# A macaron encoder block: the third chunk of the second feed-forward in two token spans, preloaded function tables, other load rates in the ordering model

## The chip, the cores and the metric

The kernel runs on one core of a Trainium2 chip. The metric is the device time of one execution in microseconds (us). TensorE (PE) multiplies, VectorE (DVE), ScalarE (ACT) and GpSimd (POOL) do the rest, SyncE (SP) issues most of the DMA transfers. Each engine takes its instructions in a fixed order.

## The reference

One layer of a bidirectional encoder on 512 tokens of width 1024, in float32. Two feed-forwards of half weight stand around a mixer of two attention groups, each between two RMS norms.

```python
def swiglu(h, w_gu, w_down):
    gate, up = jnp.split(h @ w_gu, 2, axis=-1)      # 1024 -> 2 x 2816
    return (jax.nn.silu(gate) * up) @ w_down        # 2816 -> 1024

f = swiglu(rms_norm(h, ffn1_pre_g), ffn1_w_gu, ffn1_w_down)
h = h + 0.5 * rms_norm(f, ffn1_post_g)
z = rms_norm(h, mix_pre_g) @ w_in
q_na, k_na, v_na, c_q, c_kv, k_rope = jnp.split(z, split_at, axis=-1)
o_na = neighbourhood_attention(q_na, k_na, v_na, na_rpb)           # 8 heads of 64
o_mla = latent_attention(c_q, c_kv, k_rope, ..., cos, sin)          # 8 heads, softmax over 512 keys
mixed = concatenate([rms_norm(o_na, na_out_norm_g), rms_norm(o_mla, mla_out_norm_g)]) @ w_out
h = h + rms_norm(mixed, mix_post_g)
f = swiglu(rms_norm(h, ffn2_pre_g), ffn2_w_gu, ffn2_w_down)
h = h + 0.5 * rms_norm(f, ffn2_post_g)
```

## The kernel before

**Numbers as pairs.** Every matrix operand is held as two parts, hi (rounded to the matmul's type) and lo (the rest). `split` (line 333) makes them: ScalarE copies to hi, VectorE or GpSimd subtracts to lo. `load_w` (342) loads a weight tile of 128 x 1024 into one of three staging tiles (the ring `raws`) and splits it into a ring of four hi and four lo tiles (`his`, `los`), unless a place is given in `to`. `mm3` (351) makes three matmuls of each product: hi hi, hi lo, lo hi.

**The feed-forward.** `ffn` (392) is called twice. Its 22 chunks of 128 hidden columns each have a gate half (u = 0) and an up half (u = 1). The first `direct` chunks (six in the first call, three in the second) are computed directly by `gate_up` (405), each half into its own PSUM bank, (4 + 2c + u) mod 8, over a list of token spans; the others by `winograd` (460), with fewer products on sums of quarters, whose operands `operands` (434) prepares. Then the products come back through DRAM and `down` (535) multiplies them with the second weight. `load_gu` (399) loads and splits a chunk's two weight tiles. `after` (499) adds what follows a chunk: the next chunk's weights, the sums for the Winograd part, its first operands. In the first call the tokens are there from the start, and the row norms of x are worked out beside chunks 0 and 1: four loads of token tiles, squares on ScalarE, an inverse root on GpSimd and a small matmul with a diagonal for each (lines 678 to 686). In the second call chunks 0 and 1 run over two spans, tokens 256 to 511 first, then 0 to 255; the other chunks take all 512 tokens in one matmul.

**Between mixer and second feed-forward.** The queries and keys of the latent attention lie in `Q_AT` (793) and `kbuf`. `mla_pair(j, hf)` (1041) does heads 2j and 2j + 1 for half of the tokens. Then `w_out_b` (1102) does the second half of the output projection for one token tile n, in the order 2, 3, 0, 1; its product goes to two PSUM banks (from bank 5 on, for tile 1 from bank 0 on). The norm chain that follows is: scale and add (VectorE), square with a sum (ScalarE, into a scratch area in memory), inverse root (GpSimd), multiply, scale and add, a second square and root, scale, then eight transposes on TensorE (`put_xT`, 374) and a split.

**The order.** Nothing is issued directly. `Plan.add` (111) records each operation with its dependencies, found from the addresses that it reads and writes, and with a modelled duration: for a DMA its bytes over a rate that depends on the run length, for a matmul its columns, for the other engines a fixed part and a part for each column. `Plan.place` (151) is a list scheduler forwards and backwards over these costs, with a lock between VectorE and GpSimd operations on SBUF, a slower TensorE after a long idle time, and a limit on SP's backlog of DMA. `Plan.issue` (220) repeats it six times and emits the operations in the order of the best modelled start times. So any change of a cost can move any instruction.

Of the kernel before, what the change touches and what calls it, by code (L numbers as in the profile page):

```python
# [14 lines left out]
AF = mybir.ActivationFunctionType  # L15
# [5 lines left out]
S = 512  # L21
# [6 lines left out]
EPS = 1e-6  # L28
# [15 lines left out]
class Plan:  # L44
# [66 lines left out]
    def add(self, eng, op, a, k):  # L111
        is_ap = lambda x: hasattr(x, "ap") and hasattr(x, "offset")
        outs = [x for x in (*a[:1], k.get("out"), k.get("accum_out")) if x is not None and is_ap(x)]
        ins = [x for x in (*a[1:], *(v for n, v in k.items() if n not in ("out", "accum_out"))) if is_ap(x)]
        n, deps = len(self.ops), set()
        for x in ins:
            for key, runs in self.runs(x):
                for lo, hi in runs:
                    self.touch(n, key, lo, hi, key[0] == "psum", deps)
        for x in outs:  # L120
            for key, runs in self.runs(x):
                for lo, hi in runs:
                    self.touch(n, key, lo, hi, True, deps)
        cols = max(math.prod(c for _, c in list(x.ap)[1:]) for x in outs[:1] + ins)
        kind = lambda x: x.tensor.name.rsplit("_", 1)[0]
        size = math.prod(c for _, c in list(outs[0].ap))
        big = [x for x in ins if math.prod(c for _, c in list(x.ap)[1:]) > 1]
        in_sb = sum(kind(x) != "psum" for x in big)
        tail, lock, dma = self.TAIL.get(eng, 0), False, 0
        if op == "dma_start":  # L130
            run = min(list(x.ap)[-1][1] for x in (outs[0], ins[0]))
            dma = 4 * size / (380 if run >= 1024 else 320 if run >= 512 else 230 if run >= 256 else 180 if run >= 128 else 60)
            busy, tail = (330 if eng == "SP" else 400 if eng == "ACT" else 1000), 0
        elif eng == "PE":
            busy = max(109, (cols + 32) / 2.4) * (1 + (op == "matmul" and a[1].dtype == F32))
            tail += cols / 2.4 - busy
        else:
            fix, per = {"ACT": (190, 0.834) if in_sb else (132, 0.872), "DVE": (140, 1.045), "POOL": (90, 1.0)}[eng]
            if ALU.pow in a:
                fix, per = 390, 160  # L140
            elif eng == "POOL" and in_sb > 1:
                fix, per = (130, 2.2) if cols > 256 else (300, 1.2)
            fix += 90 * (AF.Exp in a) + 45 * (op == "scalar_tensor_tensor")
            if k.get("accum_out") is not None:
                fix += 195 if eng == "ACT" else 75
            busy = fix + per * cols - tail
            in_psum = sum(kind(x) == "psum" for x in big + outs)
            lock = in_sb > 1 or in_sb and (eng == "POOL" or not in_psum and eng == "DVE")
        self.ops.append((eng, op, a, k, deps, busy, tail, lock, dma))
# [92 lines left out]
def r_(ap):  # L242
    return ap.bitcast(F32R)
# [3 lines left out]
def hybrid_block(ctx, tc, A, out):  # L247
    nc = tc.nc
    plan = Plan(tc)
    ACT, DVE, POOL, PE, SP = (plan.engine(e) for e in ("ACT", "DVE", "POOL", "PE", "SP"))  # L250
# [38 lines left out]
    gbuf, scr = big[:, :2048], big[:, 2048:]  # L289
# [6 lines left out]
    bst = Ring([new(8) for _ in range(8)])  # L296
# [8 lines left out]
    def reg(o, n):  # L305
        assert R0 + o + n <= NCOL - N32
        return mem[:, R0 + o : R0 + o + n]
# [34 lines left out]
    def load_w(src, n=1024, eng=DVE, raw=None, to=None):  # L342
        raw = fetch(src, n) if raw is None else raw
        hi, lo = to or (his.get()[:, :n], los.get()[:, :n])
        split(hi, lo, raw, eng)
        return hi, lo
# [14 lines left out]
    def row_rms(src, scratch, scale, eps, st=stat):  # L361
        s = st.get()
        ACT.activation(scratch, src, AF.Square, scale=scale, accum_out=s[:, 0:1])
        DVE.tensor_scalar(s[:, 1:2], s[:, 0:1], eps, None, ALU.add)
        return rstd(s[:, 1:2], st)
# [26 lines left out]
    def ffn(w_gu, w_dn, gpost, on_tile, L, first, resid, mid_tile=None, rs=None):  # L392
# [6 lines left out]
        def load_gu(c):  # L399
            for u in range(2):  # L400
                i = 2 * c + u
                hi, lo = load_w(w_gu[i])
                ws[c, u] = (hi.rearrange("p (k j) -> p k j", k=KD), lo.rearrange("p (k j) -> p k j", k=KD))

        def gate_up(cs, spans, nxt):
            pb = {(c, u): bank((4 + 2 * c + u) % 8) for c in cs for u in range(2)}
            for i, (t0, t1) in enumerate(spans):
                for c in cs:
                    order = [(k, u) for u in range(2) for k in range(KD)]
                    for k, u in sorted(order) if c in by_k else order:  # L410
                        wh, wl = ws[c, u]
                        mm3(pb[c, u][:, t0:t1], (wh[:, k, :], wl[:, k, :]), xt(k, t0, t1),
                            k == 0 and i == 0, k == KD - 1 and i == len(spans) - 1)
            nxt()
            for c in cs:
                tm = L["tmp"].get()
                sil, g = tm[:, :512], tm[:, 512:]
                if rs is None:
                    ACT.activation(sil, pb[c, 0], AF.Silu)
                else:  # L420
                    DVE.tensor_tensor(sil, pb[c, 0], rs, ALU.mult)
                    ACT.activation(sil, sil, AF.Silu)
                    DVE.tensor_tensor(sil, sil, rs, ALU.mult)
                DVE.tensor_tensor(g, pb[c, 1], sil, ALU.mult)
                SP.dma_start(gdr[c], g)
# [73 lines left out]
        def after(c):  # L499

            if 0 < c < direct - 1:
                load_gu(c + 1)
            for f in steps.get(c, ()):
                f()
            if c == direct - 1:
                operands(direct)

        by_k = ()
        if rs is None:
            load_gu(0)  # L510
            load_gu(1)
            gate_up((0, 1), [(t, t + 256) for t in first], lambda: after(1))
        else:
            ws, by_k = first, (0, 1)
            gate_up((0,), [(0, S)], lambda: after(0))
            gate_up((1,), [(0, S)], lambda: after(1))
        for c in range(2, direct):
            gate_up((c,), [(0, S)], lambda: after(c))
        for c in range(direct, NFC):
            winograd(c)  # L520


        slots, last_w = ([reg(o, 1024) for o in x] for x in (L["slots"], L["last_w"]))
# [39 lines left out]
        for n in range(NT):  # L563
            s = stat.get()
            t = ts.get()
# [152 lines left out]
    def scale(k):  # L718
# [9 lines left out]
    L1 = {  # L728
        "tmp": Ring([h[0], h[1]]), "sums": (hall[:, :2048], hall[:, 2048:]),
        "sets": (reg(22528, 7168), reg(0, 7168), his_los), "B": B1, "steps": steps1, "direct": 6,  # L730
        "order": lambda c: 1 if c < 8 else (c + 1) % 2,
        "slots": [1024 * i for i in range(7)] + [8192 + 1024 * i for i in range(6)]
        + [26624 + 1024 * i for i in range(4)] + [7168] + [14336 + 1024 * i for i in range(4)],
# [368 lines left out]
    def w_out_b(n, b0, hr):  # L1102
        t = slice(n * P, (n + 1) * P)
        mx = h[n]
        SP.dma_start(hr, h1[n * P : (n + 1) * P, :])
        ps = psum[:, b0 * 512 : b0 * 512 + 1024]
        for j in range(4):
            oh, ol = oT[4 + j]
            for hf in range(2):
                c = slice(hf * 512, hf * 512 + 512)  # L1110
                mm3(ps[:, c], (oh[:, t], ol[:, t]), (wb[j][0][hf], wb[j][1][hf]), j == 0, j == 3)
        DVE.scalar_tensor_tensor(mx, ps, rB[:, n : n + 1], mx, ALU.mult, ALU.add)
        sq = reg(Q_AT[6] + 256, 1)
        sq = r_(bass.AP(tensor=sq.tensor, offset=sq.offset, ap=[sq.ap[0], [Q_AT[4] - Q_AT[6], 2], [512, 2], [1, 256]]))
        r = row_rms(mx.rearrange("p (a b c) -> p a b c", a=2, b=2), sq, 1.0 / 32, EPS, bst)
        DVE.tensor_tensor(mx, mx, gp, ALU.mult)
        DVE.scalar_tensor_tensor(mx, mx, r, hr, ALU.mult, ALU.add)
        SP.dma_start(h2[n * P : (n + 1) * P, :], mx)
        r = row_rms(mx.rearrange("p (a b c) -> p a b c", a=2, b=2), sq, 1.0 / 32, EPS, bst)
        DVE.scalar_tensor_tensor(hr, mx, r, gn, ALU.mult, ALU.mult)  # L1120
        put_xT(n, hr, (2, 3), mx)

# [20 lines left out]
    w_out_b(2, 5, raws.get())  # L1143
    mla_pair(3, 0)
    w_out_b(3, 5, raws.get())
    o_rstd(1, (0, 1))
    w_out_b(0, 5, tmps.get())
    w_out_b(1, 0, tmps.get())
# [2 lines left out]
    def after2(n, t):  # L1151
# [11 lines left out]
    L2 = {  # L1163
        "tmp": cut(1024, 3), "sums": (hall[:, :2048], gbuf),
        "sets": (reg(12288, 7168), reg(19456, 7168), his_los), "B": B2, "steps": steps2, "direct": 3,
        "order": lambda c: c % 2,
        "slots": [19456 + 1024 * i for i in range(7)] + [4096 + 1024 * i for i in range(15)],
        "last_w": (19456, 20480),
# [71 lines left out]
```

## Time and profile before

| | us |
|---|---|
| median of 3 runs | 953.15 (950.69 to 956.06) |
| the profiled execution | 952.66 |
| its span, first to last instruction | 950.9 |
| TensorE busy in it | 935.2 |
| VectorE busy | 692.1 |
| ScalarE busy | 477.5 |
| GpSimd busy | 300.7 |

Mean granted clock of TensorE: 0.996 of full speed. In the first 200 us or so the first gate and up products run, from there to about 330 us the first down products, then the mixer to about 604 us; the second feed-forward fills the rest, and the last matmul ends at about 943 us. Matmuls overlap in TensorE's pipeline, so a busy TensorE is not yet one at its peak; what it does in a stretch is better seen by the number of matmuls of a shape in a window. All tiles of one memory have one name in the trace (m, memr, psum), and all instructions are recorded by one helper line (L238), so instructions are told apart by engine, operation, shape and time.

### The profile page before, as it was taken

The numbers are of one execution on the slowest core, as the hardware profiler recorded it, in microseconds if no ns is written. First come the engines' busy times: TensorE is split into PE (matmuls) and PEld (weight loads), VectorE is DVE, ScalarE is ACT, GpSimd is POOL, SyncE is SP. The second block draws the span as 40 slices with busy tenths as digits, with TensorE's granted clock in tenths as the row PEclk, the third lists the DMA queues.
The fourth block names the chain that finished last, engine by engine and source line by source line (L and its number), as shares of the span: only waits on it lengthen the run. The fifth ranks groups of instructions, "written<-read, shape, count | busy, mean of one in ns | idle before, by whom it ended". The sixth has DMA issues, their size and how long they took to land. (4 is left out here: it accounts for less than half of the span.)

```text
span 950.9 us, 15283 instructions
## 1 busy us (share of the span) xinstructions
PE 935.2 (98%) x5882; PEld 845.2 (89%) x5882; DVE 692.1 (73%) x978; ACT 477.5 (50%) x848; POOL 300.7 (32%) x232
## 2 busy tenths in 40 slices
PE   9999999999999999999999999899999999999996
PEld 7789999999888888889988888899999999988885
DVE  5899999997522376587797678899999997642224
ACT  5545554544421353588777866655454544432122
POOL 0005668650000013222452323139687761000000
PEclk9999999999999999999999999999999999999999
DMA  9635444478742456113281115354444346743212
GB/s 269 229 120 176 134 135 141 135 206 261 212 120 88 125 185 131 45 53 69 93 188 42 45 54 169 109 176 148 138 131 144 123 149 209 252 148 95 89 45 89
DMA packets 61897, 130.11 MB, mean 137 GB/s; under 512 B 21888, under 2 KB 23808, under 8 KB 61824
## 3 DMA queue, kind: packets, MB, share of 16 engines
q1 hardware_dynamic: 60672, 127.30, 43.9%
q0 software_dynamic: 1008, 1.84, 1.2%
q8 instruction: 46, 0.75, 0.3%
q14 instruction: 27, 0.22, 0.1%
q10 hardware_dynamic: 144, 0.00, 0.0%
HBM read 109.45 MB, written 17.83 MB: 134 GB/s over the span
## 5 line engine op out<-in xcount | busy, mean ns | idle before, releaser
L238 PE MATMUL psum<-memr 128*128 128x256 f32 (+3 forms) x5524 | 914.0, 326 | 0.8 <-DVE memr L238 0.5
L238 PEld LDWEIGHTS psum<-memr 128*128 128x128 f32 x5524 | 805.8, 191 | 81.7 <-ACT memr L238 2.9
L238 DVE TENSOR_TENSOR memr<-m,memr 128x1024 fp32r<-128x1024 f32 (+3 forms) x314 | 365.7, 1184 | 146.7 <-ACT memr L238 145.0
L238 POOL TENSOR_TENSOR m<-m 128x512 f32<-128x512 f32 (+5 forms) x193 | 265.5, 1391 | 562.9 <-DVE m L238 414.6
L238 ACT CAST memr<-m 128x512 fp32r<-128x512 f32 (+1 forms) x321 | 264.6, 841 | 303.4 <-PE psum L238 193.2
L238 DVE TENSOR_TENSOR m<-psum,m 128x512 f32<-128x512 f32 (+3 forms) x176 | 109.4, 624 | 31.6 <-ACT m L238 21.0
L238 DVE TENSOR_TENSOR memr<-psum,memr 128x512 fp32r<-128x512 f32 (+3 forms) x116 | 67.8, 603 | 23.1 <-ACT memr L238 22.0
L238 ACT CAST memr<-psum 128x512 fp32r<-128x512 f32 (+2 forms) x124 | 62.8, 524 | 38.8 <-PE psum L238 29.7
L238 PE MATMUL psum<-m 128*128 128x128 f32 (+1 forms) x358 | 56.9, 277 | 7.5 <-DVE m L238 6.4
L238 PEld LDWEIGHTS psum<-m 128*128 128x128 f32 x358 | 45.2, 154 | 16.2 <-DVE m L238 5.6
L238 ACT ACTIVATE m<-psum 128x256 f32<-128x256 f32 (+2 forms) x62 | 27.4, 443 | 55.9 <-PE psum L238 32.2
L238 DVE TENSOR_TENSOR psum<-psum,m 128x256 f32<-128x256 f32 (+1 forms) x78 | 44.0, 574 | 4.5 <-PE psum L238 3.5
L238 ACT ACTIVATE m<-m 128x256 f32<-128x256 f32 (+3 forms) x78 | 36.4, 467 | 20.7 <-DVE m L238 20.4
L238 DVE SCALAR_TENSOR_TENSOR m<-m 128x512 f32<-128x512 f32 (+1 forms) x36 | 33.7, 968 | 4.9 <-POOL m L238 4.3
L238 DVE TENSOR_TENSOR m<-m 128x512 f32<-128x512 f32 (+2 forms) x42 | 34.7, 836 | 0.8 <-ACT m L238 0.3
L238 ACT COPY m<-psum 128x256 f32<-128x256 f32 (+3 forms) x72 | 30.8, 432 | 8.7 <-PE psum L238 7.5
L238 ACT ACTIVATE m<-psum,m 128x512 f32<-128x512 f32 x40 | 26.9, 687 | 10.1 <-DVE m L238 7.1
L238 ACT ACTIVATE memr<-m 128x512 fp32r<-128x512 f32 (+2 forms) x28 | 21.0, 759 | 14.4 <-DVE m L238 11.3
L238 POOL TENSOR_TENSOR memr<-m,memr 128x1024 fp32r<-128x1024 f32 x8 | 19.3, 2414 | 14.1 <-ACT memr L238 12.5
L238 POOL CAST memr<-memr 64x512 fp32r<-64x512 f32 x8 | 5.9, 741 | 51.4 <-DVE memr L238 51.4
L238 DVE TENSOR_REDUCE m<-psum 128x1 f32<-128x512 f32 x32 | 21.1, 682 | 0.0
L238 DVE TENSOR_SCALAR m<-m 128x1 f32<-128x1 f32 (+1 forms) x36 | 6.5, 179 | 19.0 <-ACT m L238 10.5
(24 smaller groups left out, 95.5 us busy)
## 6 DMA issues: line engine op xcount, KB each, us to landing
m<-in_ffn_w_gu SPq DMA_DIRECT2D x86, 512.0 KB
m<-in_ffn_w_down SPq DMA_DIRECT2D x44, 512.0 KB
gd<-m SPq DMA_DIRECT2D x44, 256.0 KB
m<-gd SPq DMA_DIRECT2D x44, 256.0 KB
m<-in_x SPq DMA_DIRECT2D x8, 512.0 KB
m<-in_w_qk SPq DMA_DIRECT2D x8, 512.0 KB
h<-m SPq DMA_DIRECT2D x8, 512.0 KB
m<-in_w_out SPq DMA_DIRECT2D x8, 512.0 KB
```

Source lines behind the costliest of these rows:

```text
L238: r = getattr(self.engines[eng], op)(*a, **k)
```

## The change

The diff, whole:

```diff
--- before.py
+++ after.py
@@ -129,7 +129,7 @@
         tail, lock, dma = self.TAIL.get(eng, 0), False, 0
         if op == "dma_start":
             run = min(list(x.ap)[-1][1] for x in (outs[0], ins[0]))
-            dma = 4 * size / (380 if run >= 1024 else 320 if run >= 512 else 230 if run >= 256 else 180 if run >= 128 else 60)
+            dma = 4 * size / (300 if run >= 1024 else 280 if run >= 512 else 230 if run >= 256 else 180 if run >= 128 else 60)
             busy, tail = (330 if eng == "SP" else 400 if eng == "ACT" else 1000), 0
         elif eng == "PE":
             busy = max(109, (cols + 32) / 2.4) * (1 + (op == "matmul" and a[1].dtype == F32))
@@ -140,7 +140,7 @@
                 fix, per = 390, 160
             elif eng == "POOL" and in_sb > 1:
                 fix, per = (130, 2.2) if cols > 256 else (300, 1.2)
-            fix += 90 * (AF.Exp in a) + 45 * (op == "scalar_tensor_tensor")
+            fix += 90 * (AF.Exp in a) + 1280 * (cols == 1 and (AF.Exp in a or AF.Silu in a)) + 45 * (op == "scalar_tensor_tensor")
             if k.get("accum_out") is not None:
                 fix += 195 if eng == "ACT" else 75
             busy = fix + per * cols - tail
@@ -399,7 +399,7 @@
         def load_gu(c):
             for u in range(2):
                 i = 2 * c + u
-                hi, lo = load_w(w_gu[i])
+                hi, lo = load_w(w_gu[i], **L["own"].get(i, {}))
                 ws[c, u] = (hi.rearrange("p (k j) -> p k j", k=KD), lo.rearrange("p (k j) -> p k j", k=KD))
 
         def gate_up(cs, spans, nxt):
@@ -507,17 +507,21 @@
 
         by_k = ()
         if rs is None:
+            spans = [(t, t + 256) for t in first]
             load_gu(0)
             load_gu(1)
-            gate_up((0, 1), [(t, t + 256) for t in first], lambda: after(1))
+            gate_up((0, 1), spans, lambda: after(1))
+            gate_up((2,), spans, lambda: after(2))
         else:
             ws, by_k = first, (0, 1)
             gate_up((0,), [(0, S)], lambda: after(0))
             gate_up((1,), [(0, S)], lambda: after(1))
-        for c in range(2, direct):
-            gate_up((c,), [(0, S)], lambda: after(c))
+            for c in range(2, direct):
+                gate_up((c,), [(0, S)], lambda: after(c))
         for c in range(direct, NFC):
             winograd(c)
+        if rs is not None:
+            ACT.activation(scr[:, 0:1], ups.items[(ups.i - 1) % 2][:, 0:1], AF.Exp)
 
 
         slots, last_w = ([reg(o, 1024) for o in x] for x in (L["slots"], L["last_w"]))
@@ -728,6 +732,7 @@
     L1 = {
         "tmp": Ring([h[0], h[1]]), "sums": (hall[:, :2048], hall[:, 2048:]),
         "sets": (reg(22528, 7168), reg(0, 7168), his_los), "B": B1, "steps": steps1, "direct": 6,
+        "own": {4 + u: {"to": (reg(22528 + 2048 * u, 1024), reg(23552 + 2048 * u, 1024))} for u in range(2)},
         "order": lambda c: 1 if c < 8 else (c + 1) % 2,
         "slots": [1024 * i for i in range(7)] + [8192 + 1024 * i for i in range(6)]
         + [26624 + 1024 * i for i in range(4)] + [7168] + [14336 + 1024 * i for i in range(4)],
@@ -1110,13 +1115,13 @@
                 c = slice(hf * 512, hf * 512 + 512)
                 mm3(ps[:, c], (oh[:, t], ol[:, t]), (wb[j][0][hf], wb[j][1][hf]), j == 0, j == 3)
         DVE.scalar_tensor_tensor(mx, ps, rB[:, n : n + 1], mx, ALU.mult, ALU.add)
-        sq = reg(Q_AT[6] + 256, 1)
-        sq = r_(bass.AP(tensor=sq.tensor, offset=sq.offset, ap=[sq.ap[0], [Q_AT[4] - Q_AT[6], 2], [512, 2], [1, 256]]))
-        r = row_rms(mx.rearrange("p (a b c) -> p a b c", a=2, b=2), sq, 1.0 / 32, EPS, bst)
+        sq = reg(14336, 1)
+        sq = r_(bass.AP(tensor=sq.tensor, offset=sq.offset, ap=[sq.ap[0], [2048, 2], [1, 512]]))
+        r = row_rms(mx.rearrange("p (a c) -> p a c", a=2), sq, 1.0 / 32, EPS, bst)
         DVE.tensor_tensor(mx, mx, gp, ALU.mult)
         DVE.scalar_tensor_tensor(mx, mx, r, hr, ALU.mult, ALU.add)
         SP.dma_start(h2[n * P : (n + 1) * P, :], mx)
-        r = row_rms(mx.rearrange("p (a b c) -> p a b c", a=2, b=2), sq, 1.0 / 32, EPS, bst)
+        r = row_rms(mx.rearrange("p (a c) -> p a c", a=2), sq, 1.0 / 32, EPS, bst)
         DVE.scalar_tensor_tensor(hr, mx, r, gn, ALU.mult, ALU.mult)
         put_xT(n, hr, (2, 3), mx)
 
@@ -1143,6 +1148,7 @@
     w_out_b(2, 5, raws.get())
     mla_pair(3, 0)
     w_out_b(3, 5, raws.get())
+    ACT.activation(scr[:, 0:1], half.items[3][:, 0:1], AF.Silu)
     o_rstd(1, (0, 1))
     w_out_b(0, 5, tmps.get())
     w_out_b(1, 0, tmps.get())
@@ -1163,6 +1169,7 @@
     L2 = {
         "tmp": cut(1024, 3), "sums": (hall[:, :2048], gbuf),
         "sets": (reg(12288, 7168), reg(19456, 7168), his_los), "B": B2, "steps": steps2, "direct": 3,
+        "own": {4: {"to": (reg(20480, 1024), reg(24576, 1024)), "eng": POOL}},
         "order": lambda c: c % 2,
         "slots": [19456 + 1024 * i for i in range(7)] + [4096 + 1024 * i for i in range(15)],
         "last_w": (19456, 20480),
```

In words. (1) The model of DMA takes 300 and 280 instead of 380 and 320 bytes a nanosecond for long runs, and 1280 ns more for a ScalarE operation on one column with Exp or Silu. (2) In the second call the third chunk (c = 2) runs over the two spans of 256 tokens as well, gate and up half. Its gate half's weights (tile 4) get a place of their own, at 20480 and 24576, and GpSimd makes their lo part; 20480 was the query of head 4, 24576 its key. (3) In the first call both tiles of the third chunk get a place of their own, in the area of the first Winograd operands. (4) A one-column Exp is issued after the last chunk of the first call, a one-column Silu after the last attention pair. (5) The scratch of the squares in `w_out_b` moves from the queries of heads 6 and 4 to the place that holds the key of head 5.

## Rows read from the trace of the kernel before

**Rows 1.** The page's busy table: busy us (share of the span) xinstructions.

```profile
PE 935.2 (98%) x5882; PEld 845.2 (89%) x5882; DVE 692.1 (73%) x978; ACT 477.5 (50%) x848; POOL 300.7 (32%) x232
```

**Rows 2.** Windows: us, busy us (xinstructions) per engine, granted clock, DMA share, GB/s.

```profile
100.00:200.00 100.00, 100.00 (x835) 100.00 (x835) 98.49 (x105) 50.62 (x82) 70.22 (x43) 1.00 0.44 143
200.00:285.00 85.00, 85.00 (x516) 76.44 (x515) 47.98 (x63) 32.66 (x51) 5.62 (x4) 1.00 0.71 202
900.00:938.00 38.00, 38.00 (x169) 31.45 (x169) 12.57 (x16) 8.58 (x15) 1.10 (x2) 1.00 0.17 55
```

**Rows 3.** Timeline of TensorE: start us, us, instruction, xcount [idle before <-releaser].

```profile
25.78 0.49 PE L238 MATMUL psum<-m 128*128 128x128 f32 x2 [0.62 <-DVE m L238]
28.34 0.49 PE L238 MATMUL psum<-m 128*128 128x128 f32 x2 [0.92 <-DVE m L238]
...
397.64 0.44 PE L238 MATMUL psum<-m 128*128 128x128 f32 x2 [1.11 <-ACT m L238]
...
468.67 1.44 PE L238 MATMUL psum<-m 128*128 128x128 f32 x12 [0.96 <-DVE m L238]
...
606.50 1.06 PE L238 MATMUL psum<-m 128*128 128x128 f32 x8 [2.49 <-DVE m L238]
```

**Rows 4.** Windows of one us at the second feed-forward's entry, TensorE alone.

```profile
604.00:605.00 1.00, 0.01 (x1) 1.00 0.71 295
...
608.00:609.00 1.00, 0.81 (x5) 0.65 0.00 0
609.00:610.00 1.00, 1.00 (x5) 0.50 0.70 143
...
611.00:612.00 1.00, 1.00 (x8) 0.64 0.11 25
```

**Rows 5.** Grouped by shape: TensorE 588 to 597.2 us, then 597.4 to 604.1.

```profile
L238 PE MATMUL psum<-memr 128*128 128x256 f32 x51 | 6.4, 283 | 0.0
...
L238 PE MATMUL psum<-memr 128*128 128x256 f32 x45 | 5.9, 287 | 0.3 <-DVE memr L238 0.3
```

**Rows 6.** Timeline of the last tiles' norm chain, VectorE, then GpSimd.

```profile
592.10 1.28 DVE L238 SCALAR_TENSOR_TENSOR m<-psum,m 128x1024 f32<-128x1024 f32 x1
...
599.66 1.22 DVE L238 TENSOR_TENSOR m<-m 128x1024 f32<-128x1024 f32 x1
...
605.07 1.28 DVE L238 SCALAR_TENSOR_TENSOR m<-m 128x1024 f32<-128x1024 f32 x1 [0.44 <-POOL m L238]
...
597.80 0.55 POOL L238 TENSOR_TENSOR m<-m 128x1 f32<-128x1 f32 x1 [2.83 <-DVE m L238]
599.88 1.40 POOL L238 TENSOR_TENSOR m<-m 128x1 f32<-128x1 f32 x1 [1.53 <-DVE m L238]
```

**Rows 7.** Timeline of ScalarE at the end of the mixer.

```profile
557.83 0.69 ACT L238 ACTIVATE m<-psum,m 128x512 f32<-128x512 f32 x1
...
564.93 1.06 ACT L238 ACTIVATE memr<-m 128x1024 fp32r<-128x1024 f32 x1 [3.14 <-DVE m L238]
...
574.16 1.07 ACT L238 CAST memr<-psum 128x512 fp32r<-128x512 f32 x2 [1.95 <-PE psum L238]
```

**Rows 8.** Timeline: a GpSimd split of 1024 columns, then SP's weight loads.

```profile
523.57 2.40 POOL L238 TENSOR_TENSOR memr<-m,memr 128x1024 fp32r<-128x1024 f32 x1 [3.86 <-ACT memr L238]
...
585.29 2.44 SPq L238 DMA_DIRECT2D m<-in_ffn_w_gu  x3
...
597.49 0.33 SPq L238 DMA_DIRECT2D m<-in_ffn_w_gu  x1
...
608.19 0.33 SPq L238 DMA_DIRECT2D m<-in_ffn_w_gu  x1
```

**Rows 9.** Timeline of ScalarE at the first exponential.

```profile
395.70 1.28 ACT L238 ACT_TABLE_LOAD   x1
396.99 0.51 ACT L238 ACTIVATE m<-m 128x256 f32<-128x256 f32 x1
```

**Rows 10.** The windows view, 15 to 20 us.

```profile
15.00:20.00 5.00, 5.00 (x24) 4.14 (x23) 3.06 (x5) 3.07 (x5) 0.00 (x0) 1.00 1.06 234
```

## Prediction, made before the change was run

> **What bounds the kernel now.** I read the page's busy table first: TensorE is busy 935.2 us of a span of 950.9 us [rows 1]. The profiled run took 952.66 us, 1.76 us around the span, and lies 0.5 us under the 953.15 us median. So only three things can change the time: a stretch in which TensorE has nothing to do, a lower granted clock, and a change in what its matmuls cost. Second, the windows view gives their cost: 835 matmuls of 256 columns in 100 us are 119.8 ns each, with the weight loads busy all of it; 169 matmuls of 512 columns in 38 us are 224.9 ns each [rows 2]. Third, the timeline of TensorE alone, for every line that carries an idle time. Between 5 us and the last matmul there are nine such gaps: 0.62 and 0.92 us in the first feed-forward, 1.11 us at the first softmax, 0.96, 0.38 and 0.34 us in the mixer and behind it (the first of the three is shown), and 2.49, 0.24 and 0.19 us at the entry of the second feed-forward (again the first is shown) [rows 3]. That is 7.25 us. Fourth, the windows of that entry: the clock is at its upper level (2.4 GHz) until TensorE has stood idle from 604.0 to 606.5 us and done eight transposes, then at the lower (1.2 GHz) from about 608.3 to 611.6 us (of the two windows at 0.50 one is shown) [rows 4]. The shares missing in these four windows (0.35, 0.50, 0.50, 0.36 of a microsecond) cost 1.7 us. Nothing else inside the kernel can be won: 9 us in all, below 1%.
>
> **Why TensorE stops at 604.0 us.** Chunks 0 and 1 of the second feed-forward have 2 x 2 x 24 = 96 matmuls on tokens 256 to 511. The grouped view counts 51 before 597.2 us and 45 after [rows 5]: all 96 are done at 604.0. The next work needs token tile 1, the last one, whose norm chain ends with a VectorE step from 605.07 to 606.35 us [rows 6]. TensorE, in its fixed order, waits for it.
>
> **The change, part by part.**
> *Third chunk in two spans.* Its 48 matmuls of 512 columns become 96 of 256. By the rows this costs 48 x (2 x 119.8 - 224.9) = 0.70 us. The page "TensorE: Matmul & The Clock Gate" of the Trainium skill (Back-to-back issue gap) gives a streamed matmul its columns plus a fixed part of 2.5 ns; estimated from that, the doubling would cost 48 x 2.5 ns = 0.1 us, and the sum below would be 0.6 us better. The rows' 119.8 ns contradict that.
> *What fills the gap.* The gate half's first span is 24 matmuls, 24 x 119.8 = 2.88 us, which need tokens 256 to 511 only. They need PSUM bank 0: it is read out by the VectorE step at 592.10 us, 1.28 us long [rows 6], so it is free by 593.4. They need their split weights. The own place holds head 4's query and key, last used by pair (2, 0), whose last exponential starts at 557.83 us [rows 7]. The split is 1.05 us on ScalarE and 2.40 us on GpSimd [rows 8]. The raw weights need one of three staging tiles; the queue loads weights in a burst of three at 585.29, then at 597.49 and 608.19 us [rows 8]. By the order of the ring, the third chunk's gate weights are either in the burst or come at 608.19, after a staging tile that is free from about 592.2. Nothing in the rows keeps the load from going there; even with the 597.49 slot, with some 3 us to land and 3.5 to split, it would be ready at 604. The load moves ahead of a store or two on SP; SP is idle for most of this stretch. So of 2.49 + 0.24 + 0.19 = 2.92 us of idle I take 2.6 away: what is late next is tile 1 itself, as 604.0 + 2.88 = 606.9 is 0.4 us past its chain's end. Bounds: 0 (weights late) and 2.9.
> *The clock.* With no idle longer than the 1.11 us ahead of the first softmax, where no window shows a lower clock, the 1.7 us comes back; I take 1.6, bounds 0 and 1.7.
> *Removed from VectorE.* One split of 1024 columns goes to GpSimd, behind 608 us, where TensorE streams without a gap: nothing.
> *Exponential's table.* The load takes 1.28 us at 395.70; the first exponential starts at 396.99 and TensorE's transposes at 397.64, after 1.11 us of idle [rows 3, 9]. The exponential starts as the load ends, so it waits for nothing else; without the load it starts up to 1.29 us earlier, and the idle goes: 1.1 us, bounds 0 and 1.1. The load moves behind the last chunk of the first feed-forward, where TensorE is busy 85.00 us of 85 and ScalarE 32.66 [rows 2]: nothing.
> *Silu's table.* Its load at 614.09 stands where TensorE has no gap: nothing is won. Moved behind the last exponential of the mixer, it meets a wait of 1.95 us of ScalarE on TensorE that ends at 574.16 [rows 7]: nothing is lost. If that cover is gone, 1.3 us.
> *New scratch of the norm squares.* It lies on head 5's key, last read by pair (2, 0): its last exponential is at 557.83, the first square at 564.93 [rows 7]. No wait.
> *Own place in the first feed-forward, and the load rates.* No instruction is added; the planner's order changes everywhere. The model takes 300 instead of 380 bytes a ns. The rows give 234 at 15 to 20 us, while the token tiles come in, with the DMA engines full [rows 10]; so the old model put the four token loads too early, and the two small matmuls that need the third and fourth stand in TensorE's order before their inputs are there: 0.62 and 0.92 us [rows 3]. A later estimate moves them behind other matmuls (eight of 0.22 us were left). But the bytes still have to arrive, so I take 0.6 of 1.54. Bounds: 1.5 won, and 1.0 lost, as the 0.96 us gap [rows 3] is what one badly placed wait costs.
> *Sum.* -2.6 - 1.6 + 0.7 - 1.1 - 0.6 = -5.2 us: 952.66 becomes 947.5, and the median 953.15 becomes **948.0**.
>
> **The rivals.**
> *The weights come late.* If the planner keeps the load at 608.19 or the split behind the gap, TensorE waits as before and the third chunk only costs 0.7: 953.15 + 0.7 - 1.1 - 0.6 = 952.1. For it: in the kernel before, the chunk's splits follow 608 us. Against it: the places are free early, and the planner sees the gap.
> *GpSimd's split in the norm chain (slower).* GpSimd also computes the inverse roots of this chain. The one at 597.80 takes 0.55 us; the one at 599.88, issued while VectorE runs a two-input step (599.66, 1.22 us), takes 1.40 us and ends behind that step [rows 6]: the two engines exclude each other. A split of 2.40 us placed ahead of a root of tile 1 therefore can hold the root 2.4 us, and a two-input VectorE step as much again: 4.8 us. The chain would end at 611.2; TensorE would idle 611.2 - 606.9 = 4.3 us instead of 2.9, the clock would fall as before: +1.4 + 0.7 - 1.1 - 0.6 = +0.4, 953.6. If the order elsewhere gains nothing and loses the 1.0 above, it is 955.2. It decides from the point at which the delay passes some 2.5 us. "SBUF — State Buffer" of the Trainium skill (the shared port pair) states just this: an exclusive lock, held for the whole instruction. By that rule a single collision costs one 2.4 us; the 1.40 us row agrees. Against the rival: GpSimd is idle from 594.98 to 597.80, long enough for the split.
> *A new stall from the new order (slower).* A stall like the present one costs 2.9 + 1.7 = 4.6 us. One anywhere in the kernel brings the forecast back to 952.6; together with late weights 956.7.
> *The start is won in full.* With both gaps gone (1.5) and no hand-over loss (2.9): 946.8.
> *The tables aren't moved.* If the planner puts a preload ahead of the last function of the old set, the tables are loaded again, and 1.1 us stay: 949.1.
>
> **How the numbers follow.** Forecast and its neighbours with parts of the small terms (946 to 949.5) 0.58; start won in full (945 to 947) 0.10; weights late or half late (949.5 to 952.5) 0.18; a collision or new stall that eats the gain (952 to 958) 0.14. The measurement tells about 0.5% (4.8 us) from no change, so faster means below 948.4. The forecast of 948.0 sits at that edge: of its 0.58 I count 0.37 below it, and with the start 0.47; slower, above 957.9, 0.04; same 0.49. Range 944.8 to 952.8: the lower end is every term at its better bound (-2.9 - 1.7 + 0.7 - 1.1 - 1.5 = -6.5, 946.6) with the three mixer gaps of 1.7 gone too, the upper takes in the late weights.
>
> **What would show it.** In the changed trace: 24 matmuls of 256 columns between 604 and 607 us, no idle of TensorE above 0.5 us there and a granted clock of 1.00 throughout 600 to 620; a GpSimd split of about 2.4 us between 592 and 604; table loads still three, the exponential's between 200 and 330 us, no idle at the first softmax; gaps near 25 and 28 us smaller. The prediction is wrong if a gap of 2 us or a clock window below 1.00 remains between 590 and 620, or if gaps over 1 us appear where there were none.

## The result and the profile after

| | before | changed |
|---|---|---|
| median, us | 953.41 (950.69 to 956.06, 7 runs) | 947.98 (946.18 to 949.77, 7 runs) |
| ratio | | 0.9942, 95% interval 0.9923 to 0.996 |
| the profiled execution, us | 952.66 | 949.77 |
| its span | 950.9 | 948.0 |
| TensorE's idle in it, 20 us to the last matmul | 7.25 | 2.40 |

The kernel is 0.6% faster; 948.0 was forecast. The two profiled executions differ by only 2.9 us, because the changed kernel's is the slowest of its seven runs: TensorE's clock fell in it at a place where it had not fallen in the profile of before, and for longer.

The timeline of TensorE in the changed kernel (start us, us, instruction, xcount [idle before <-releaser]):

```profile
28.97 0.49 PE L238 MATMUL psum<-m 128*128 128x128 f32 x2
30.10 2.12 PE L238 MATMUL psum<-memr 128*128 128x512 f32 x8 [0.18 <-DVE memr L238]
...
395.66 0.38 PE L238 MATMUL psum<-m 128*128 128x128 f32 x2
...
466.63 2.02 PE L238 MATMUL psum<-m 128*128 128x128 f32 x12 [0.98 <-DVE m L238]
...
607.30 1.06 PE L238 MATMUL psum<-m 128*128 128x128 f32 x8 [0.66 <-DVE m L238]
```

Against [rows 3]: the waits of the small matmuls near 25 and 28 us (0.62 and 0.92) are gone, and one of 0.18 for a split on VectorE stands behind them; the transposes of the first softmax follow without the 1.11 us; the wait near 466 us is the same; the 2.49 us at the entry of the second feed-forward are 0.66, and the 0.24 and 0.19 behind them are gone. Two gaps of 0.37 and 0.21 us near 574 and 589 us aren't shown.

Grouped by shape, TensorE from 587.5 to 607.2 us:

```profile
L238 PE MATMUL psum<-memr 128*128 128x256 f32 x114 | 14.2, 283 | 0.0
```

Where [rows 5] added up to 96 matmuls of 256 columns there are 114 ahead of the last tile's transposes: 18 of the third chunk's gate half. The other six stand behind the transposes, while the tile is split.

Windows (us, TensorE busy (xinstructions), granted clock, DMA share, GB/s) at the two places where the clock matters, first two of the kernel before, then those of the changed one:

```profile
465.00:470.00 5.00, 4.04 (x31) 1.00 0.35 108
470.00:475.00 5.00, 5.00 (x29) 1.00 0.36 108
...
465.00:470.00 5.00, 4.02 (x24) 0.73 0.31 104
470.00:475.00 5.00, 5.00 (x19) 0.59 0.64 211
...
605.00:610.00 5.00, 4.34 (x36) 1.00 0.10 43
610.00:615.00 5.00, 5.00 (x44) 1.00 0.01 3
```

Against [rows 4]: at the entry the clock stays at its upper level (2.4 GHz). It falls instead behind 466 us, where it had stayed up before, and costs 0.27 x 5 + 0.41 x 5 = 3.4 us there.

ScalarE's table loads, and the timeline of GpSimd and VectorE around the new split:

```profile
236.16 1.28 ACT L238 ACT_TABLE_LOAD   x1
578.32 1.28 ACT L238 ACT_TABLE_LOAD   x1
```

```profile
591.51 2.41 POOL L238 TENSOR_TENSOR memr<-m,memr 128x1024 fp32r<-128x1024 f32 x1 [0.51 <-ACT memr L238]
593.88 1.53 POOL L238 TENSOR_TENSOR m<-m 128x1 f32<-128x1 f32 x1
...
593.66 1.34 DVE L238 TENSOR_TENSOR m<-m 128x1024 f32<-128x1024 f32 x1
```

The exponential's load lies in the first feed-forward, Silu's in the mixer ([rows 9] had the first at 395.70). GpSimd's split ends at 593.92, just as tile 0's chain needs its root; VectorE's two-input step takes 1.34 us instead of the 1.22 of [rows 6].

### The profile page after: what moved, and what is told of

Its sections match the earlier page's. It is cut to its first block, busy times and chain, and to the rows that moved or that the text cites. A ratio compares the mean times of both kernels' runs of the same rounds, so it can differ in the third digit from the quotient of the medians.

```text
span 948.0 us, 15333 instructions
## 1 busy us (share of the span) xinstructions
PE 937.1 (99%) x5930; PEld 850.5 (90%) x5930; DVE 693.6 (73%) x977; ACT 477.9 (50%) x850; POOL 289.6 (31%) x233
## 5 line engine op out<-in xcount | busy, mean ns | idle before, releaser
L238 PE MATMUL psum<-memr 128*128 128x256 f32 (+2 forms) x5572 | 914.5, 324 | 0.4 <-ACT memr L238 0.2
L238 POOL TENSOR_TENSOR m<-m 128x512 f32<-128x512 f32 (+5 forms) x193 | 252.1, 1321 | 567.6 <-DVE m L238 397.4
L238 ACT CAST memr<-m 128x1024 fp32r<-128x1024 f32 (+1 forms) x321 | 265.1, 841 | 277.2 <-PE psum L238 167.8
L238 PE MATMUL psum<-m 128*128 128x128 f32 (+1 forms) x358 | 59.3, 285 | 3.1 <-DVE m L238 3.1
L238 PEld LDWEIGHTS psum<-m 128*128 128x128 f32 x358 | 47.9, 162 | 11.1 <-DVE m L238 3.6
L238 DVE TENSOR_TENSOR psum<-psum,m 128x512 f32<-128x512 f32 (+1 forms) x78 | 42.8, 571 | 6.4 <-PE psum L238 5.4
L238 POOL TENSOR_TENSOR memr<-m,memr 128x1024 fp32r<-128x1024 f32 x9 | 21.6, 2409 | 14.6 <-ACT memr L238 13.0
```

What stands on the lines that cost most here:

```text
L238: r = getattr(self.engines[eng], op)(*a, **k)
```

## The experiments

Each was timed against the kernel before on the same chip; the ratio has its 95% interval. TensorE's idle in the one profiled execution of each, in us, by place (start: 20 to 31 us; entry: behind 600 us). "Clock" is what the shares missing from the granted clock cost in that execution up to the last matmul, "span" its length:

| | start | first softmax | 466 us | other | entry | sum | clock | span | ratio |
|---|---|---|---|---|---|---|---|---|---|
| before | 1.54 | 1.11 | 0.96 | 0.72 | 2.92 | 7.25 | 1.7 | 950.9 | 1 |
| changed | 0.18 | 0 | 0.98 | 0.58 | 0.66 | 2.40 | 3.4 | 948.0 | 0.9942 |
| spans only (e1) | 0.66 | 1.12 | 0.96 | 0.36 | 1.29 | 4.39 | 1.7 | 948.6 | 0.9982 |
| no spans (e2) | 0 | 0 | 0.97 | 0.60 | 2.88 | 4.45 | 1.7 | 948.5 | 0.9977 |
| tables only (e3) | 2.00 | 0 | 0.93 | 0.78 | 3.28 | 6.99 | 1.7 | 950.7 | 0.9996 |
| rates only (e4) | 0 | 1.12 | 0.94 | 0.70 | 3.00 | 5.76 | 1.7 | 949.4 | 0.9997 |
| split on VectorE (e5) | 0.63 | 0 | 0.85 | 1.12 | 0.34 | 2.94 | 1.7 | 947.7 | 0.9956 |
| four more chunks (e6) | 1.07 | 0 | 0.97 | 1.52 | 0.70 | 4.26 | 0 | 949.5 | 0.9973 |
| other banks (e7) | 0.18 | 0 | 0.78 | 0.89 | 0.66 | 2.51 | 0 | 945.7 | 0.9942 |
| no own place (e8) | 0.25 | 0 | 0.97 | 0.59 | 0.65 | 2.46 | 1.7 | 946.2 | 0.9943 |
| before again (e9) | 1.71 | 1.11 | 0.93 | 0.72 | 3.01 | 7.48 | 1.7 | 952.2 | |
| fillers (e10) | 0.53 | 0 | 0 | 0.57 | 0.68 | 1.78 | 0 | 945.7 | 0.9942 |
| changed again (e11) | 0.74 | 0 | 0.94 | 0.59 | 0.68 | 2.95 | 1.7 | 946.9 | 0.9939 |

The idle, the clock and the price of shorter matmuls (0.68 us a chunk, see e6) explain the spans: taken off, they leave 941.4 to 942.5 us in twelve of the thirteen profiles (in e10 with 1.1 us for its fillers) and 943.0 in e9. So what the change gained is idle that went, less the price of the spans; the clock made its own difference in each execution.

**e1, the spans alone.** On the kernel before:

```diff
-            gate_up((0, 1), [(t, t + 256) for t in first], lambda: after(1))
+            gate_up((0, 1), spans, lambda: after(1))
+            gate_up((2,), spans, lambda: after(2))
...
+        "own": {4: {"to": (reg(20480, 1024), reg(24576, 1024)), "eng": POOL}},
```

> The kernel before with one part of the change: the third chunk of the second feed-forward in two spans, its gate half's own place with the split on GpSimd, and the scratch that has to move for it. Theory (the gap at the entry is filled and the clock stays up there): 3.5 us less than before, 953.4 becomes about 949.9; no idle of TensorE above 0.7 us between 590 and 612 us, granted clock 1.00 in that stretch; the idle of 1.1 us at the first exponential and the two of 0.6 and 0.9 us near 25 and 28 us stay. Rival (the gain came from the new order of the whole kernel, not from the spans): within 1 us of before.

Measured: 951.11 us, ratio 0.9982 (0.9973 to 0.999), 1.7 us less, half of what the theory wanted. The last tile's inverse root on GpSimd, and TensorE at the entry:

```profile
604.97 1.40 POOL L238 TENSOR_TENSOR m<-m 128x1 f32<-128x1 f32 x1 [3.33 <-DVE m L238]
...
607.84 1.07 PE L238 MATMUL psum<-m 128*128 128x128 f32 x8 [1.13 <-DVE m L238]
610.15 1.10 PE L238 MATMUL psum<-memr 128*128 128x256 f32 x7 [0.16 <-DVE memr L238]
```

The gap is filled, but not as well as in the changed kernel: VectorE runs a weight split (604.75, 1.22 us) beside the last tile's root, which takes 1.40 us instead of 0.86 in the changed kernel; the chain ends later, and 1.13 us stay. In all 2.86 us of idle are gone and 0.68 us are paid for the spans (e6): 2.2 us, within the interval of the 1.7. The clock brought nothing here: it fell once in this profile too, behind 466 us.

**e2, all but the spans.** On the changed kernel:

```diff
-            gate_up((2,), spans, lambda: after(2))
...
-            for c in range(2, direct):
-                gate_up((c,), [(0, S)], lambda: after(c))
+        for c in range(2, direct):
+            gate_up((c,), [(0, S)], lambda: after(c))
```

> The changed kernel without that part: the third chunk in one matmul of 512 columns again, the old weight ring and the old scratch; tables, rates and the first feed-forward's own place stay. Theory: the gap of about 2.5 us near 606 us is back, and the lower clock behind it; 951.5 (3.5 us above the changed kernel, 1.7 to 2 us below before). Rival (order): about 948.

Measured: 950.46 us, ratio 0.9977 (0.9965 to 0.9988). The gap is back:

```profile
605.28 1.07 PE L238 MATMUL psum<-m 128*128 128x128 f32 x8 [2.24 <-DVE m L238]
```

Beside the rest of the change the spans are thus worth 0.9977 - 0.9942 = 0.35%, 3.3 us: the theory's 3.5, and the rival is out, since the two intervals don't meet. But the theory's reason holds only in part. The lower clock didn't come with the gap:

```profile
605.00:610.00 5.00, 4.08 (x31) 1.00 0.47 166
610.00:615.00 5.00, 5.00 (x44) 1.00 0.12 47
465.00:470.00 5.00, 4.03 (x25) 0.78 0.28 95
470.00:475.00 5.00, 5.00 (x25) 0.88 0.64 211
```

The idle sums give 4.45 - 2.40 - 0.68 = 1.4 us for the spans; where the other 1.9 of the 3.3 us come from isn't shown. The intervals of the two ratios are wide enough, about 2 us together, that it can be noise.

**e3, the tables alone.** On the kernel before:

```diff
+            fix += 90 * (AF.Exp in a) + 1280 * (cols == 1 and (AF.Exp in a or AF.Silu in a)) + 45 * ...
+            ACT.activation(scr[:, 0:1], ups.items[(ups.i - 1) % 2][:, 0:1], AF.Exp)
+    ACT.activation(scr[:, 0:1], half.items[3][:, 0:1], AF.Silu)
```

> The kernel before with the two one-column activations and their modelled cost alone. Theory: the exponential's table load moves to about 230 us, the idle of 1.11 us at the first exponential goes, the Silu load moves ahead of 590 us and changes nothing; 1.1 us less than before, 952.3. Rival (ScalarE's load is hidden anyway, or another wait takes its place): within 0.3 us of before, with a new idle behind 397 us.

Measured: 952.33 us, ratio 0.9996 (0.9982 to 1.0009). The 1.11 us at the first softmax are gone, but not the time:

```profile
29.09 0.49 PE L238 MATMUL psum<-m 128*128 128x128 f32 x2 [2.00 <-DVE m L238]
...
606.35 1.06 PE L238 MATMUL psum<-m 128*128 128x128 f32 x8 [3.04 <-DVE m L238]
```

The idle at the start has grown from 1.54 to 2.00 us, and that at the entry from 2.92 to 3.28, in an order that the planner made anew. 1.11 were won and 0.85 given back, all places taken together. The edit does what it says; what it is worth depends on the order that comes with it.

**e4, the rates alone.** On the kernel before:

```diff
-            dma = 4 * size / (380 if run >= 1024 else 320 if run >= 512 ...
+            dma = 4 * size / (300 if run >= 1024 else 280 if run >= 512 ...
```

> The kernel before with the new load rates in the model alone. Theory: the small matmuls of the token norms come later in TensorE's order, the idles of 0.62 and 0.92 us near 25 and 28 us go or shrink to under 0.3 us together; 0.6 to 1.5 us less, 952.3. The gap near 606 us stays. Rival (the bytes set the pace): the same idle appears as a wait of the third chunk's first matmuls for its weights, time unchanged.

Measured: 951.74 us, ratio 0.9997 (0.9987 to 1.0006). All idle at the start is gone (1.54 to 0), no new wait takes its place, and the profiled span is 949.4 us, 1.5 less; the median is 1.0 less, the ratio says nothing within its interval of 1.8 us. The trace bears the theory out, the time can't confirm it. Windows of the same execution:

```profile
605.00:610.00 5.00, 3.23 (x24) 1.00 0.16 42
610.00:615.00 5.00, 5.00 (x44) 1.00 0.53 173
465.00:470.00 5.00, 4.05 (x28) 0.83 0.33 105
470.00:475.00 5.00, 5.00 (x23) 0.83 0.62 211
```

Here the gap at the entry is 2.49 us, as in [rows 3], and the clock stays at its upper level; it fell behind 466 us.

**e5, the split on VectorE.** On the changed kernel:

```diff
-        "own": {4: {"to": (reg(20480, 1024), reg(24576, 1024)), "eng": POOL}},
+        "own": {4: {"to": (reg(20480, 1024), reg(24576, 1024))}},
```

> The changed kernel with the gate half's split on VectorE instead of GpSimd. Theory (GpSimd's 2.4 us lie where neither the chain's roots nor VectorE wait for them): VectorE's 1.2 us now stand in or beside the norm chain, the idle at the entry of the second feed-forward grows from 0.66 to 1 to 2 us; 0.5 to 1.3 us more than the changed kernel, about 949. Rival (the shared port costs the chain what GpSimd's split holds it): the idle shrinks below 0.66 us, 947. Whatever the order does elsewhere is read from TensorE's idle in the same trace and taken off.

Measured: 949.14 us, ratio 0.9956 (0.9938 to 0.9973), within the noise of e8 on the same chip (0.9943). The median is the one that the theory names, but its step fell: the idle at the entry is smaller, not larger.

```profile
607.21 1.06 PE L238 MATMUL psum<-m 128*128 128x128 f32 x8 [0.34 <-DVE m L238]
```

VectorE splits from 592.85 to 594.07 us, ahead of tile 0's chain; the steps behind it are in a tighter order (594.05 to 607.05 us instead of 593.66 to 607.15). GpSimd's split costs the chain only the 0.12 us by which VectorE's step was longer. Four runs each don't show which engine splits better, and no run splits late, so what an early split is worth isn't shown.

**e6, four more chunks in two spans.** On the changed kernel:

```diff
             for c in range(2, direct):
-                gate_up((c,), [(0, S)], lambda: after(c))
+                gate_up((c,), [(0, 256), (256, S)], lambda: after(c))
```

> The changed kernel with the third to sixth chunk of the first feed-forward in two spans of 256 tokens as well, where this fills no gap: 192 matmuls of 512 columns become 384 of 256. By the rows of before (119.8 and 224.9 ns) it costs 4 x 0.70 = 2.8 us: 950.8. If a matmul of 256 columns costs just half of one of 512 plus 2.5 ns, it costs 0.5 us: 948.5.

Measured: 950.13 us, ratio 0.9973 (0.9962 to 0.9983), 0.30% or 2.9 us above e8 in the same session. That this is the 2.8 us forecast is chance: between the two profiles the idle grew by 1.8 us, and the clock, which fell in e8 and not here, gave 1.7 back. So the time alone doesn't measure the rate. The rate itself is in the windows of 32 to 72 us (engines in the order of [rows 2]), of the kernel with four more chunks and then of the changed one:

```profile
32.00:72.00 40.00, 40.00 (x335) 40.00 (x335) 39.62 (x48) 18.62 (x22) 0.00 (x0) 1.00 0.50 162
```

```profile
32.00:72.00 40.00, 40.00 (x178) 33.10 (x178) 39.49 (x48) 19.94 (x24) 0.00 (x0) 1.00 0.49 160
```

335 matmuls of 256 columns are 119.4 ns each, 178 of 512 are 224.7: 48 x (2 x 119.4 - 224.7) = 0.68 us a chunk. Every matmul has a weight load of its own, and with 256 columns some load is under way in all 40 us, with 512 in 33.1. But one load lasts about as long in both, 192 and 188 ns in the mean, so the loads overlap one another, and whether they set the pace of the short matmuls isn't shown.

**e7, other banks for two transposes.** On the changed kernel:

```diff
-        b = bank(nb())
+        b = bank((0, 1, 6, 7)[n])
```

> The changed kernel with the transposes of the first two tiles of the latent projections in PSUM banks 0 and 1 instead of 6 and 7, so that they needn't wait until the last two products have been read out of banks 6 and 7. Theory: the idle of 0.98 us near 466 us shrinks below 0.4 us, and the clock no longer falls behind it in some of the runs (3.4 us in the profiled run of the changed kernel); 946.5, with less spread between runs. Rival (the last tile's own chain sets the time): the idle stays at 0.9 to 1.0 us and the time at 948.

Measured: 947.38 us, ratio 0.9942 (0.9929 to 0.9956). The theory's idle below 0.4 us didn't come; as the rival has it, a wait stays, 0.78 us long, and only moved behind the transposes.

```profile
465.86 3.21 PE L238 MATMUL psum<-m 128*128 128x2 f32 x28
469.85 0.50 PE L238 MATMUL psum<-memr 128*128 128x512 f32 x1 [0.78 <-ACT memr L238]
```

The windows from 460 to 475 us are at 1.00 in this execution, and its six runs lie within 1 us (947.17 to 948.11); six are too few to call that an effect.

**e8, no own place in the first feed-forward.** On the changed kernel:

```diff
-        "own": {4 + u: {"to": (reg(22528 + 2048 * u, 1024), reg(23552 + 2048 * u, 1024))} for u in range(2)},
+        "own": {},
```

> The changed kernel without the third chunk's own place in the first feed-forward. Theory (the start was won by the later estimate of the loads alone): TensorE's order is the same instruction for instruction, idle up to 30 us below 0.3 us, time within 1 us of the changed kernel. Rival (the place is needed at the start): an idle of 0.5 us or more near 29 us, where the third chunk's first matmuls wait for their weights' split.

Measured: 948.0 us, ratio 0.9943 (0.9923 to 0.9963). TensorE's matmuls follow in the same order of shapes, its idle up to 31 us is 0.25. The place is worth nothing that can be seen.

**e9, before again.** No edit.

> The kernel before once more, unchanged, for its trace alone. Theory (whether the clock falls behind a given stretch of little work differs from execution to execution): the idle of TensorE stands at the same places with the same lengths, but the windows below 1.00 need not: near 466 to 475 us, near 606 to 612 us, at both or at neither. Rival (the 2.49 us gap always costs its 1.7 us): the clock falls at 608 us as in the first trace.

Measured: 954.0 us. Idle as in the first trace of before. Windows:

```profile
465.00:470.00 5.00, 4.10 (x30) 1.00 0.55 196
470.00:475.00 5.00, 4.97 (x33) 1.00 0.20 56
...
605.00:610.00 5.00, 2.08 (x15) 0.97 0.19 80
610.00:615.00 5.00, 4.91 (x30) 0.69 0.33 108
```

The clock fell at the entry, as in [rows 4], 1.7 us. This trace alone doesn't part the theory from the rival; e2 and e4 do, whose gap of 2.24 and 2.49 us left the clock up.

**e10, fillers in the wait near 466 us.** On the changed kernel, in the loop that issues (nothing else moves; the five products are not used):

```diff
+            [... self.engines["PE"].matmul(*self.filler[1], start=True, stop=True, ...) for _ in range(5 * (i == self.filler[0]))]
...
+        if n == 0:
+            plan.filler = len(plan.ops), (bank(0), r_(xt(0, 0, P)[0]), r_(xt(1, 0, S)[0]))
```

> The changed kernel with five matmuls of 512 columns (1.1 us, their result is not used) put into TensorE's order ahead of the transposes that wait 0.98 us near 466 us; everything else keeps its place. Theory (the clock falls behind the stretch of tiny matmuls, idle and transposes there, in some executions): the fillers lie in the idle, cost 0.1 to 0.3 us, and no window from 460 to 480 us is below 1.00; the median falls by 1 to 2 us against the changed kernel on the same chip, to 946 to 947, and its slowest runs go. Rival (idle alone counts): no change, or 0.2 us more.

Measured: 947.32 us, ratio 0.9942 (0.993 to 0.9954). They lie where they should:

```profile
466.02 1.41 PE L237 MATMUL psum<-memr 128*128 128x512 f32 x5
467.26 1.39 PE L238 MATMUL psum<-m 128*128 128x128 f32 x12
```

The window from 465 to 470 us is at 1.00. But there is no gain over e11 beside it (0.9939): the theory's 1 to 2 us didn't come, the rival's "no change" did. The mean clocks agree: of the thirteen profiled executions the ten with a fall report 0.995 to 0.997, the three without one 0.998 or 0.999. In both kernels four of six runs are at 0.998, so in these runs the fillers made falls no rarer.

**e11, the changed kernel again.** No edit.

> The changed kernel once more, unchanged, beside the run with the fillers and the kernel before on the same chip. 947.0 to 948.5; the trace shows the same idle as the first one (2.4 us in all behind 30 us), and a clock that falls near 466 us or nowhere.

Measured: 946.83 us, ratio 0.9939 (0.9926 to 0.9952). The clock fell near 466 us in the profiled execution (948.65 us, the slowest of six); the idle at the start is 0.74 instead of 0.18, since the loads land at other times (ScalarE's squares of the first token tile, which wait for its load, start at 20.10 us instead of 18.52). So a term of half a microsecond at the start can't be told from one trace.

## Why the prediction was right

The forecast's time was met within 0.1 us, and that is luck: the terms for the gap and the clock were taken 0.9 to 1.3 us too large, those for the start and the other gaps 0.5 to 0.9 too small. The price of the spans was right, the gap nearly so. By its own steps:

| term | forecast, us | measured |
|---|---|---|
| third chunk fills the gap | -2.6 | -2.26 (2.92 to 0.66) |
| clock at the entry | -1.6 | -0.6 to -1.0 for the clock at any place, from the runs' mean clocks |
| two spans instead of one | +0.7 | +0.68 (e6) |
| exponential's table | -1.1 | -1.11 |
| start | -0.6 | -1.0 to -1.4 |
| other gaps | 0 | -0.1 |
| sum | -5.2 | -4.4 to -5.2 by these terms; -5.4 between the medians |

*The gap.* Right in mechanism and size; the reason for what stays was wrong. I expected TensorE to come 0.4 us late for the last tile; it still waits 0.66 us for it, because the planner put six of the 24 matmuls behind the transposes, where the two short waits had been. So two of the named signs were missed in part: 18 matmuls instead of 24 ahead of the transposes, and 0.66 us of idle instead of 0.5 at most.

*The clock.* This step failed in its reason and was oversized. It took the fall behind the 2.49 us gap for certain; e2 has a gap of 2.24 us and e4 one of 2.49 with the clock up. And it took an idle of up to 1.11 us for harmless; behind 0.98 us near 466 us the clock fell in the changed kernel's own profile, and cost 3.4 us. Mean clocks tell how often it falls: 49 of 63 runs of before are at 0.997 or below, where every profile had a fall (see e10), and 7 of 13 runs of the changed kernel. The medians are 0.996 (0.992 to 0.999) and 0.997 (0.995 to 0.998). A thousandth is worth 0.95 us of full rate, and 0.6 us by the slope of time on clock over the 63 runs. At like clock the kernels can be compared without it: at 0.998 the medians are 951.6 (8 runs) and 946.8 (6), at 0.997 952.5 (9) and 947.9 (4). So 4.6 to 4.8 us of the gain are not the clock's; the runs are of several sessions, and few.

*The price of the spans.* The rows' 0.70 held: e6 measures 0.68. The 0.1 us against it was an estimate from the fixed part of 2.5 ns on "TensorE: Matmul & The Clock Gate" of the Trainium skill (Back-to-back issue gap). What the prediction left out is the limit that this section sets to it: in a stream of weight loads and matmuls the formula counts too little at small N and too much at large N (its examples are 128 and 512 columns). Here it counts too little at both lengths: as estimates it gives 109.2 and 215.8 ns, and e6's windows show 119.4 for 256 columns and 224.7 for 512.

*The tables.* Right for the first exponential in the changed kernel, and Silu's load brought nothing, as written. e3 adds what I left out: by itself the edit shifts the order, and most of the gain went elsewhere.

*The start.* Undersized: I took 0.6 of 1.54 us, since "the bytes still have to arrive". They do arrive in time; the waits came from order alone. e4 and e8 show it: the rates alone remove all of it, the own place adds nothing. Each is one trace, and e11 shows that the landing of the loads moves this term by half a microsecond.

*The rivals.* Late weights: out, the split is done at 593.92, ten microseconds ahead of its use. GpSimd in the chain: the split overlaps VectorE's step by 0.26 us and costs 0.12. The collision is real, though: in e6 the split ends at 595.42, the two overlap by 0.78 us, and the step takes 1.87 us instead of 1.22; in both cases it ends 1.1 us behind the split. That the two engines shut each other out, as "SBUF — State Buffer" of the Trainium skill (Terms, shared port pair) says, agrees with these rows, but it decided nothing: the planner kept the overlap short. A new stall from the new order: not in the changed kernel; e3 shows that it is real (0.85 us given back). Tables not moved: out, both loads moved and there are still three.

The parts don't add up one by one: alone they give 0.18% (e1), 0.04% (e3) and 0.03% (e4), together 0.58%. The idle sums say why: 7.25 becomes 4.39, 6.99 and 5.76 with one part each, since each leaves or lengthens the waits of the others, and 2.40 with all. Not settled: 0.5 us between the sum of the terms at like clock (idle -4.85, spans +0.68: -4.2) and the 4.6 to 4.8 measured; it lies within the intervals. (The lower end of the forecast's range adds up to 944.9, not 944.8.)

## What to carry to other kernels

In a kernel whose main engine is busy 98% of the time, list that engine's gaps one by one: as long as its own work stays the same, their sum and what the lower clock costs bound what a change can bring. Here idle, clock and the price of shorter matmuls together gave every profile's difference from the span of before to within 1.1 us. Work for a gap should be priced at the measured rate of the shape that it is cut into. With a planner that orders everything, judge an edit in the order that it makes, and read its worth from the idle sum of that trace, not from the one wait that it removes.

## What the runs showed of the hardware that was not expected

The fall of TensorE's clock is not a fixed property of a gap. Behind an idle of 2.24 to 3.04 us near 606 us it fell in three profiled executions (before, e3, e9) and stayed up in two (e2, e4). Behind 0.95 us of tiny matmuls, 0.85 to 0.98 us of idle and transposes near 466 us it fell in seven (e1, e2, e4, e5, e8, the changed kernel twice) and stayed up in four with 0.93 to 0.97 (before, e3, e6, e9). None of these executions had both falls, so the gain at the entry may be lost again at another place, as in the changed kernel's first profile. What decides between them is not known; the fillers of e10 took the idle and the fall near 466 us away in one profile, but not from the time. A fall cost 1.7 us in nine profiles and 3.4 in one, and the mean clock that each run reports shows it: the median of the runs of before goes from 951.2 us at 0.999 to 955.8 at 0.992.

A matmul of 256 columns with a weight load of its own takes 119.4 ns at the upper clock against 224.7 for 512, so two short ones take 14.1 ns more than a long one.
